# A fused RMSNorm and swish: one small load issued later in ScalarE's queue

## The chip, the cores and the metric

The kernel runs on one core of one Trainium2 chip. The metric is the device time of an execution in microseconds, and a kernel's time is the median of its runs. The profile is of one execution; it has a span (first to last instruction) and an execution time that is a little longer than the span.

## What is computed

The input x has 16 x 1024 rows of 512 numbers in float32, gamma has 512 numbers. Each row is divided by the root of its mean square (plus eps), multiplied by gamma, and passed through swish.

```python
rms = np.sqrt(np.mean(x ** 2, axis=-1, keepdims=True) + eps)
x_norm = x / rms * gamma
return (x_norm * (1.0 / (1.0 + np.exp(-x_norm)))).astype(np.float32)
```

33.6 MB are read and as many written.

## The kernel before

**Tiling.** The 16384 rows are cut into 8 groups of 2048 rows, and each partition (128 of them) has 16 neighbouring rows of a group. A buffer `xb` in on-chip memory holds 6 groups in turn, so groups 6 and 7 take the places of groups 0 and 1. The work on a group goes in chunks of four rows per partition (2048 numbers), 32 chunks in all, counted here from 0. Results are written over the input in `xb` and stored from there.

**Loads.** All but one are issued by SyncE (`load`, line 111), whose DMA queue is called q1 in the profile, in this order: rows 0 to 3 of group 0, rows 4 to 7, rows 8 to 15, then rows 1 to 15 of group 1 (3840 KB), then whole groups (4096 KB) 2 to 6, and group 7 in two halves. The first two are placed ahead of all else in SyncE's program. The load of group 6 waits for the store of group 0, and that of group 7 for the store of group 1. Row 0 of group 1 (one row per partition, 256 KB, 128 pieces of 2 KB) is loaded on its own through ScalarE's DMA queue, q10 (line 185). Its landing is told by the semaphore `s_row`.

**Gamma.** POOL clears `gamma4` (line 131). Then ScalarE issues a DMA (line 187) that brings gamma (8 KB in all) to every 32nd partition, and VectorE spreads it over all partitions with a shuffle (line 228). This shuffle stands behind the first reduce in VectorE's order.

**A chunk k on the engines.** ScalarE waits for the load that holds the chunk, squares one row with an accumulating sum (line 156), and squares the other three rows into one of two PSUM buffers (line 163): this is `square(k)`. Only the first chunk of group 1, which is chunk 4, waits in addition for `s_row`. VectorE sums the three rows (line 204, `sums`). POOL adds eps and raises to the power -1/2 (lines 136 and 143). VectorE multiplies each of four rows by its factor and by gamma (line 215, `norm`). ScalarE applies Silu in place (line 175, `swish`). After the last chunk of a store's piece, ScalarE issues the store through q10 (line 180).

**The order on the engines.** Each engine's order is written out by hand. ScalarE: the row's load, gamma's load, the table load for its functions (line 190), then for each k `square(k)`, the stores that are due, `swish(k - 2)`. A store is due when its last chunk is at most k - 2; so the store of group 6 stands behind `square(30)`, which waits for the last load. VectorE: `sums(0)`, the shuffle of gamma, `sums(1)`, `norm(0)`, and so on: `sums(k)`, `norm(k - 1)`.

Of the kernel before, what the change touches and what calls it, by code (L numbers as in the profile page):

```python
# [9 lines left out]
def kernel(  # L10
# [7 lines left out]
    nc = tc.nc  # L18
# [6 lines left out]
    xf = x.flatten_outer_dims()  # L25
# [50 lines left out]
    s_row = nc.alloc_semaphore("s_row")  # L76
# [12 lines left out]
    def need(ins, sem, value):  # L89
        return ins.wait_op(sem, value, "sem-ge")  # L90

    def dram(ap, piece):
        g, r, n = piece
        rows = ap[g * P * gn : (g + 1) * P * gn]
        return rows.rearrange("(p n) d -> p n d", n=gn)[:, r : r + n, :]

    def buf(piece):
        g, r, n = piece
        at = g % ring * gn + r
        return xb[:, at : at + n, :]  # L100
# [33 lines left out]
    for k in range(K):  # L134
        need(
            nc.gpsimd.tensor_scalar(  # L136
                out=aeps[:, k, :], in0=ms[:, k, :], scalar1=eps_f, scalar2=None,
# [6 lines left out]
                out=rstd[:, k, :], in0=aeps[:, k, :], in1=neg_half, op=ALU.pow  # L144
# [5 lines left out]
    def square(k):  # L150
        at, landing = chunks[k]
        if landing is not None:
            nc.scalar.wait_ge(ld[landing], 16)  # L153
            if loads[landing][1] % cn:
                nc.scalar.wait_ge(s_row, 16)
        acc = nc.scalar.activation(  # L156
            out=junk[k % 2], in_=xb[:, at + n_sq, :], func=AF.Square,
            scale=inv_d**0.5, accum_out=ms[:, k, n_sq : n_sq + 1],
        )
        if k >= 2:  # L160
            need(acc, s_acc, k - 1)
        acc.then_inc(s_acc, 1)
        square = nc.scalar.activation(  # L163
            out=sq[k % 2][:, 0:n_sq, :], in_=xb[:, at : at + n_sq, :],
            func=AF.Square, scale=inv_d**0.5,
        )
        if k >= 2:
            need(square, s_sum, k - 1)
        square.then_inc(s_sq, 1)

    def swish(k):
        at, _ = chunks[k]
        rows = xb[:, at : at + cn, :]
        need(
            nc.scalar.activation(out=rows, in_=rows, func=AF.Silu), s_norm, k + 1  # L175
        ).then_inc(s_swish, 1)

    def store(t):
        need(
            nc.scalar.dma_start(out=dram(of, stores[t]), in_=buf(stores[t])),  # L180
            s_swish, ends[t],
        ).then_inc(st[t], 16)

    first_row = (1, 0, 1)
    nc.scalar.dma_start(out=buf(first_row), in_=dram(xf, first_row)).then_inc(s_row, 16)
    need(
        nc.scalar.dma_start(out=gamma4[0:P:32, :], in_=gamma.partition_broadcast(4)),
        s_zero, 1,
# [3 lines left out]
    for k in range(K + 3):  # L192
        if k < K:
            square(k)
        while stored < len(stores) and ends[stored] <= k - 2:
            store(stored)
            stored += 1
        if 2 <= k < K + 2:
            swish(k - 2)
# [74 lines left out]
```

## Time and profile before

| | us |
|---|---|
| median of 6 runs | 160.17 |
| lowest and highest | 160.13 and 161.01 |
| the profiled execution | 160.95 |
| its span | 159.6 |
| DVE, ACT, POOL busy in it | 138.9, 125.2, 65.5 |
| one reduce (line 204), one normalised row (line 215) | 1.75, 0.74 |
| one block of squares (line 163), one swish (line 175) | 1.43, 1.91 |
| row of group 1, issue to landing | 8.4 |
| share of DMA time taken by q10 and by q1 | 49.3% and 49.2% |

The profile is read like this. Engines are named PE (matrix, unused here), DVE (VectorE), ACT (ScalarE), POOL (GpSimd) and SP (SyncE); ACTq and SPq are their queues, which issue DMAs. L204 is line 204 of the kernel. The page gives each engine's busy time, a row of 40 equal slices of the span with a digit of busy tenths each, and the chain of work that ended last, followed back from the last instruction. Other views are the timeline, the list of DMA issues with the time from issue to landing, the waits, and a table of busy time for any stretch of the span. A DMA share of 1.00 means that all 16 DMA engines were moving packets; it can pass 1 since a packet is counted in the stretch where it starts.

### The profile page before, as it was taken

Reading aid. Unit: us, or ns where it says so; the run is one execution under the profiler, and the core shown is the slowest. Engines: PE = TensorE matmul, PEld = TensorE weight load, DVE = VectorE, ACT = ScalarE, POOL = GpSimd, SP = SyncE. Lnnn points to the kernel's source line nnn. Section 1 sums busy time; section 2 is a strip of 40 time slices with the busy share of each in tenths; the row PEclk is TensorE's granted clock in tenths of the full one; section 3 lists DMA queues with packets and bytes.
Section 4 is the critical chain, followed back from the end, with each engine's and each line's share of the span. In section 5 each row is a group of like instructions: output and inputs, shape, how many; then the busy total and the mean of one; then the engine's idle time right before and its main releaser. Section 6 shows DMA issues by size and latency. Waiting matters only on the chain.

```text
span 159.6 us, 435 instructions
## 1 busy us (share of the span) xinstructions
DVE 138.9 (87%) x162; ACT 125.2 (78%) x129; POOL 65.5 (41%) x70
## 2 busy tenths in 40 slices
DVE  0239999999999999999999999999999999699600
ACT  1835888888888889988888888888899886783810
POOL 1034444444455555544444445555554444255000
DMA  7999899999999999999999999999999898999994
GB/s 267 439 413 493 369 517 394 394 394 394 525 396 394 476 437 402 419 484 402 402 495 411 411 452 443 419 435 460 411 402 472 369 509 374 476 419 394 443 406 209
DMA packets 3035, 67.14 MB, mean 421 GB/s; under 512 B 340, under 2 KB 340, under 8 KB 472
## 3 DMA queue, kind: packets, MB, share of 16 engines
q10 hardware_dynamic: 1448, 33.83, 49.3%
q1 hardware_dynamic: 1584, 33.29, 49.2%
q14 instruction: 3, 0.02, 0.0%
HBM read 33.56 MB, written 33.55 MB: 420 GB/s over the span
## 4 chain that ended last, share of the span: by engine, by line
DVE 82%; DMA 6%; ACT 4%; issue 1%; another core or an unknown queue 1%; POOL 0%; ACTq 0%; POOLq 0%
DVE xb L215 51%; DVE ms L204 30%; DMA gamma<-in_gamma_dram 6%; ACT xb L175 2%; ACT sq L163 1%; DVE gamma_sb L228 0%; ACT junk L156 0%; POOL gamma L131 0%; ACTq L153 0%; POOLq L59 0%
## 5 line engine op out<-in xcount | busy, mean ns | idle before, releaser
L215 DVE SCALAR_TENSOR_TENSOR xb<-xb,rstd,gamma_sb 128x512 f32<-128x512 f32 x128 | 87.1, 740 | 0.0
L175 ACT ACTIVATE xb<-xb 128x2048 f32<-128x2048 f32 x32 | 61.1, 1909 | 17.6 <-DVE xb L215 17.6
L204 DVE TENSOR_REDUCE ms<-sq 128x3 f32<-128x1536 f32 x32 | 55.9, 1746 | 8.4 <-ACT sq L163 8.4
L136 POOL TENSOR_SCALAR aeps<-ms 128x4 f32<-128x4 f32 x32 | 20.7, 647 | 77.1 <-DVE ms L204 77.1
L163 ACT ACTIVATE sq<-xb 128x1536 f32<-128x1536 f32 x32 | 45.9, 1433 | 0.0
L143 POOL TENSOR_TENSOR rstd<-aeps,neg_half 128x4 f32<-128x4 f32 x32 | 44.0, 1376 | 2.7
L156 ACT ACTIVATE junk<-xb 128x512 bf16<-128x512 f32 x32 | 19.7, 615 | 5.7 <-DMA xb<-in_x_dram 5.7
L156 ACT ACTIVATION_READ_ACCUMULATOR junk<-xb 128x1 f32 x32 | 6.0, 187 | 0.0
L190 ACT ACT_TABLE_LOAD x1 | 1.3, 1283 | 3.6 <-issue 3.6
L228 DVE LOAD_MASK_SELECT gamma_sb<-gamma x1 | 0.0, 14 | 2.8 <-DMA gamma<-in_gamma_dram 2.8
L131 POOL MEMSET gamma<- 128x512 f32 x1 | 0.5, 524 | 1.5 <-POOLq L59 1.5
L228 DVE STREAM_SHUFFLE gamma_sb<-gamma 128x512 f32<-128x512 f32 x1 | 0.7, 717 | 0.0
L255 POOL MEMSET const-float32-0.0<- 128x1 f32 x1 | 0.1, 98 | 0.2 <-issue 0.2
L255 POOL MEMSET const-uint8-127<- 128x1 uint8 x1 | 0.1, 102 | 0.0
L255 POOL MEMSET const-bfloat16-1.0<- 128x1 bf16 x1 | 0.1, 101 | 0.0
L132 POOL MEMSET neg_half<- 128x4 f32 x1 | 0.1, 101 | 0.0
L255 POOL MEMSET const-float32-1.0<- 128x1 f32 x1 | 0.1, 98 | 0.0
## 6 DMA issues: line engine op xcount, KB each, us to landing
out_dram<-xb ACTq DMA_DIRECT2D x7, 4096.0 KB, 26.4
xb<-in_x_dram SPq DMA_DIRECT2D x5, 4096.0 KB, 50.8
xb<-in_x_dram SPq DMA_DIRECT2D x3, 2048.0 KB, 46.0
out_dram<-xb ACTq DMA_DIRECT2D x2, 2048.0 KB, 8.6
xb<-in_x_dram SPq DMA_DIRECT2D x1, 3840.0 KB, 19.7
xb<-in_x_dram SPq DMA_DIRECT2D x2, 1024.0 KB, 5.9
xb<-in_x_dram ACTq DMA_DIRECT2D x1, 256.0 KB, 8.4
gamma<-in_gamma_dram ACTq DMA_DIRECT2D x1, 8.0 KB
```

What stands on the lines that cost most here:

```text
L131: nc.gpsimd.memset(gamma4, 0.0).then_inc(s_zero, 1)
L132: nc.gpsimd.memset(neg_half, -0.5).then_inc(s_half, 1)
L136: nc.gpsimd.tensor_scalar(out=aeps[:, k, :], in0=ms[:, k, :], scalar1=eps_f, scalar2=None, op0=ALU.add,),
L143: nc.gpsimd.tensor_tensor(out=rstd[:, k, :], in0=aeps[:, k, :], in1=neg_half, op=ALU.pow),
L156: acc = nc.scalar.activation(out=junk[k % 2], in_=xb[:, at + n_sq, :], func=AF.Square, scale=inv_d**0.5, accum_out=ms[:, k, n_sq : n_sq + 1],)
L163: square = nc.scalar.activation(out=sq[k % 2][:, 0:n_sq, :], in_=xb[:, at : at + n_sq, :], func=AF.Square, scale=inv_d**0.5,)
L175: nc.scalar.activation(out=rows, in_=rows, func=AF.Silu), s_norm, k + 1
L190: nc.scalar.preload_act_table_set("silu_and_others")
L204: nc.vector.tensor_reduce(out=ms[:, k, 0:n_sq], in_=sq[k % 2][:, 0:n_sq, :], op=ALU.add, axis=mybir.AxisListType.X,),
L215: ins = nc.vector.scalar_tensor_tensor(out=row, in0=row, scalar=rstd[:, k, j : j + 1], in1=gamma_sb, op0=ALU.mult, op1=ALU.mult,)
L228: nc.vector.stream_shuffle(gamma_sb, gamma4, [0] * 32), s_gld, 16
L255: nc = _bacc.Bacc("TRN2", target_bir_lowering=False, num_devices=1)
```

## The change

ScalarE no longer issues the row's load first of all. It issues it behind `square(0)`, which waits for the landing of the first load; so the row comes behind gamma in the queue q10 and behind that landing in time. The row's bytes, its place, its semaphore and the chunk that waits for it stay as they were. VectorE, POOL and SyncE keep their orders. Three lines are added ahead of `sums`, so that lines from there on are numbered 3 higher, and gamma's load stands on line 186 instead of 187.

```diff
     first_row = (1, 0, 1)
-    nc.scalar.dma_start(out=buf(first_row), in_=dram(xf, first_row)).then_inc(s_row, 16)
     need(
         nc.scalar.dma_start(out=gamma4[0:P:32, :], in_=gamma.partition_broadcast(4)),
         s_zero, 1,
@@
     for k in range(K + 3):
         if k < K:
             square(k)
+        if k == 0:
+            nc.scalar.dma_start(
+                out=buf(first_row), in_=dram(xf, first_row)
+            ).then_inc(s_row, 16)
         while stored < len(stores) and ends[stored] <= k - 2:
             store(stored)
             stored += 1
```

## The prediction

> **What bounds the kernel.** I read the page first. VectorE looks like the limit, since it is busy 87% of the span and the chain that ended last gives it 82%. But the DMA row of the 40 slices is nearly all nines.
>
> ```profile
> span 159.6 us, 435 instructions
> DVE 138.9 (87%) x162; ACT 125.2 (78%) x129; POOL 65.5 (41%) x70
> DMA  7999899999999999999999999999999898999994
> HBM read 33.56 MB, written 33.55 MB: 420 GB/s over the span
> ```
>
> The table of busy time by stretches settles this (per stretch: its length, then DVE, ACT and POOL busy, clock, DMA share, GB/s):
>
> ```profile
> 1.00:34.00 33.00, 24.27 (x29) 23.14 (x27) 12.06 (x14) 1.00 1.02 429
> 36.00:135.00 99.00, 99.00 (x116) 88.50 (x92) 46.88 (x47) 1.00 1.01 433
> 135.00:152.00 17.00, 13.66 (x18) 11.51 (x10) 5.87 (x6) 1.00 0.98 423
> 152.00:153.00 1.00, 0.00 (x0) 0.06 (x1) 0.00 (x0) 1.00 0.85 360
> ```
>
> The 16 DMA engines are full from 1 us to 152, miss about 0.2 us after that, and work to 158. Those 67.1 MB are moved under either kernel. So the end is set by two things: DMA time, which the change cannot shorten, and holes in DMA work, which it can move. The idle time of VectorE at the start is not by itself on the path to the end.
>
> The chain of waits shows where each head start begins and where it dies (start, length, what):
>
> ```profile
> 2.46 8.99 DMA gamma<-in_gamma_dram
> ...
> 11.49 0.72 DVE gamma_sb L228 x2
> ...
> 133.02 1.91 ACT xb L175
> 134.93 1.64 another core or an unknown queue
> ...
> 136.65 0.42 ACT junk L156
> ```
>
> Gamma, 8 KB, takes 8.99 us, and the first normalisation stands behind it. The piece without a name at 134.93 ends at 136.57. That is the landing of the last load (issued at 75.48, 61.1 us to landing in the list of DMA issues); ScalarE waits 1.7 us for it.
>
> **Step 1: gamma lands earlier.** Its issue stays at 2.46, because it waits for POOL's memset (1.90 + 0.52 = 2.42) and not for the row. What is taken away is the row's 128 packets of 2 KB ahead of it in ScalarE's queue (q10):
>
> ```profile
> DMA packets 257, 1.71 MB, mean 428 GB/s; under 512 B 16, under 2 KB 16, under 8 KB 144
> ...
> q1 hardware_dynamic: 129, 1.45, 86.8%
> q10 hardware_dynamic: 128, 0.26, 17.3%
> ```
>
> This is the stretch 5.5 to 9.5 us: all 128 row packets lie in it, and they cost each engine 17.3% of 4 us, 0.69 us. The row, issued at 1.91, thus began 3.6 us later, ended at about 9.3 and landed 1.0 us after that, at 10.3. Gamma alone in the queue, at the same 3.6 us to its first packet and 1.0 us to landing, lands near 7.1. The bounds are 4.5 (the first load, issued at 0.0, had the engines moving after 1.0 us: 2.46 + 1.0 + 1.0) and 11.45 (no gain). Any landing before 8.72 gives the same, since the shuffle stands behind the first reduce (6.96 + 1.76).
>
> **Step 2: the front of the chain.** Shuffle 8.72 to 9.43. The second square block can start near 7.1 instead of 7.50, for the first two loads no longer share with the row: from 5.5 to 7.0 the row took 27.5% of 1.5 us, 0.4 us. Its result is ready at 9.2, so the second reduce runs from 9.43 to 11.1 and the first normalisation starts near 11.1 instead of 13.76: 2.65 us ahead.
>
> Then the loads catch up. The third load lands at 12.89 now; with the row out of part of its way, 0.3 to 0.45 us sooner. Squares then end at 12.6 + 2.06 = 14.65 and the third reduce starts at 14.7 instead of 16.40: 1.7 us ahead. The fourth load (3840 KB, issued at 2.28, 19.7 us) lands at 22.0 under both kernels, as row, gamma and loads up to it are the same bytes on full engines. Its first squares now start at 22.65; they can start at 22.1 at best. They end 2.04 later at 24.14, and the fifth reduce starts at 24.17 instead of 25.03. So of 2.65 us **0.87 us** are left, and no wait on a load follows until 134. The first store goes out near 30.5 instead of 31.40.
>
> **Step 3: the row itself.** It is issued when the first squares have started, near 4.95, beside squares that run until 6.9; its 0.40 us of issue holds nothing, as the next ScalarE instruction waits for the second load. First packets come 3.6 us later (by the row now) or 4.9 (by the first store: issued at 31.40, no q10 packet before 36): 8.5 to 9.9. Eight packets per engine take turns with packets of 0.61 to 1.14 us, at most 8 x 1.22 = 9.8 us; landing at 20.7 at the latest. It is needed at 22.1. I cost this at nothing; the cover is those 1.4 us or more, and a row later than 22.1 would only eat into the 0.87.
>
> The Trainium skill speaks against this step: "DMA: Bandwidth & Descriptors", section "Rules for kernel authors", would have a DMA issued early and waited for late, and the row is now issued 3 us later. By the rule something should be lost; by the margin above, nothing is. The same page's "Latency and other measured facts" gives about 0.6 us to the first byte on such a queue, where this trace shows 3.6 us behind a busy one; by the page gamma would be there near 4, and the sum would be the same, because of the reduce.
>
> **Step 4: what the 0.87 us does at the other end.** From 36 us both queues have work until the last load is in, and share the engines (36 to 40 us: q10 60.6%, q1 36.0%; 36.2 to 135: 56.3 and 44.4). Before that, loads have the engines to themselves. If stores begin d earlier, loads have moved d less and get about half the rate for the rest, so the last load lands about d *later*: 136.57 becomes 137.4. Packets of 32 KB last 1.21 us and take turns, so the true shift may be 0 or one turn, 1.2. From that landing to the last store is fixed work, 152.09 - 136.57 = 15.5 us; so the last store is issued d later, near 153.0.
>
> **What hides that.** At the very end one engine runs behind the others:
>
> ```profile
> 157.00:157.50 0.50, 0.00 (x0) 0.00 (x0) 0.00 (x0) 1.00 1.23 524
> 157.50:158.00 0.50, 0.00 (x0) 0.00 (x0) 0.00 (x0) 1.00 0.09 33
> 158.00:158.30 0.30, 0.00 (x0) 0.00 (x0) 0.00 (x0) 1.00 0.13 55
> 158.30:158.60 0.30, 0.00 (x0) 0.00 (x0) 0.00 (x0) 1.00 0.00 0
> 158.60:159.60 1.00, 0.00 (x0) 0.00 (x0) 0.00 (x0) 1.00 0.04 16
> ```
>
> From 157.5 only a few packets start, the last one alone after 158.6. In the trace's records of landings, 15 of the last store's 16 parts are in by 158.55 and the last at 159.59. The late engine still has the previous store's packets until about 154, so it does not notice a later issue. The 15 others do: they end at 158.55 + d. Hence the span's end is the larger of 159.59 and 158.55 + d: the cover is 1.04 us. With d = 0.87 nothing changes; with d = 1.2 it is +0.16.
>
> **Sum.** Profiled execution: 160.95, that is its span of 159.6 and 1.35 around it; predicted span 159.6 to 159.8. The median of the runs shown is 160.17, which is 0.78 less; if their late engine lags by less, the last load also lands sooner, and the cover stays. I predict 160.17 + 0.08, the middle of 0 and 0.16: **160.25 us**.
>
> **Rivals.**
> *A (forecast, 0.44).* Head start real, cut to 0.87 us by the fourth load, paid back as a later last load, hidden: 160.17 to 160.33.
> *B (slower, 0.36).* The later last load is not hidden: the last store is issued 0.87 or 1.2 us later and the DMA engines stand idle that long just before it (and also ahead of the group 6 store, which is issued behind the same landing). It decides as soon as the shift exceeds the cover; with no cover it costs all of it: 161.0 to 161.4, I take 161.0. For it: the hole at 152 to 153 (0.85) is there already. Against it: the late engine, if unprofiled runs have it.
> *C (faster, 0.12).* The head start reaches the end: 160.17 - 0.87 = 159.3. For it: VectorE has 82% of the chain and no gap from 36 to 135. Against it: DMA shares of 1.02 and 1.01, and a last load that waits for stores to share with.
> *D (does not do what it says, 0.08).* Gamma is late for another reason than the row, d = 0: 160.17.
>
> **Chances.** 0.3% is 0.48 us, about what a measurement of this kernel can tell from no change. Faster 0.12 (C), same 0.52 (A and D), slower 0.36 (B). The range 159.7 to 161.2 leaves out C and the far part of B, about 0.2; the likeliest case's own range is 160.0 to 160.4.
>
> **What would show it.** Gamma's shuffle right behind the first reduce, near 8.7 (step 1); the third reduce near 14.7 and the fifth near 24.2, behind a wait for the fourth load at 22.0 (step 2); the row landed before that (step 3); first store near 30.5, last load landing at 137 or later, last store near 153 (step 4); DMA share below 0.85 around 152 to 153 if B is right. Wrong I would be if the last load landed earlier than 136.5 with an earlier first store, if the row landed after 22, or if the late engine was gone.

## The result, and the profile after

The changed kernel takes 160.93 us (median of 27 runs, 160.34 to 161.58); the kernel before takes 160.43 in the 55 runs that now stand beside it (160.06 to 161.14). The ratio is 1.0025, with an interval of 1.0017 to 1.0034: 0.25% slower, about 0.4 us (the medians themselves lie 0.5 us apart). That is inside the 0.3% that was set as no change, and the interval reaches just past it. 160.25 was forecast, in a range of 159.7 to 161.2. Beside the experiments below, the kernel before has medians of 160.37 to 160.65, so kernels are compared by their ratios. A ratio leaves out runs over 1.5% above the fastest of their kernel; there are two of these, both of the experiment with no load in the way. Single executions of one kernel spread over some 1 us, so a single profile says little about 0.4 us: the profiled execution took 160.83, less than the 160.95 of the one before.

The page's lines after the change, to be set beside those of before:

```profile
span 159.5 us, 435 instructions
...
DVE 139.2 (87%) x162; ACT 125.3 (79%) x129; POOL 65.5 (41%) x70
...
DMA  7999899999999999999999999999999999999887
...
HBM read 33.56 MB, written 33.55 MB: 421 GB/s over the span
```

Bytes are those of before, and busy times and span differ by 0.3 us or less. What has moved is seen in the timeline (start, length, engine and line, operation, idle time before it):

```profile
4.91 0.36 ACTq L195 DMA_DIRECT2D xb<-in_x_dram  x1
...
8.67 0.72 DVE L231 STREAM_SHUFFLE gamma_sb<-gamma 128x512 f32<-128x512 f32 x1
...
14.93 1.76 DVE L207 TENSOR_REDUCE ms<-sq 128x3 f32<-128x1536 f32 x1 [1.07 <-ACT sq L163]
...
22.10 0.63 ACT L156 ACTIVATE junk<-xb 128x512 bf16<-128x512 f32 x1 [0.82 <-DMA xb<-in_x_dram]
...
24.20 1.76 DVE L207 TENSOR_REDUCE ms<-sq 128x3 f32<-128x1536 f32 x1 [0.55 <-ACT sq L163]
...
30.58 0.35 ACTq L180 DMA_DIRECT2D out_dram<-xb  x1
...
153.18 0.34 ACTq L180 DMA_DIRECT2D out_dram<-xb  x1
```

The third reduce, the fifth, the first store and the last were these in the kernel before:

```profile
16.40 1.75 DVE L204 TENSOR_REDUCE ms<-sq 128x3 f32<-128x1536 f32 x1
...
25.03 1.75 DVE L204 TENSOR_REDUCE ms<-sq 128x3 f32<-128x1536 f32 x1
...
31.40 0.35 ACTq L180 DMA_DIRECT2D out_dram<-xb  x1
...
152.09 0.34 ACTq L180 DMA_DIRECT2D out_dram<-xb  x1
```

The shuffle follows the first reduce at once. The head start is 1.5 us at the third reduce (14.93 against 16.40). The wait for the fourth load, new at 22.10, cuts it to 0.83 us at the fifth reduce and 0.82 at the first store. The chain that ended last shows where this leads:

```profile
2.27 19.76 DMA xb<-in_x_dram
...
22.10 0.72 ACT junk L156 x2
...
132.20 1.91 ACT xb L175
134.11 3.55 another core or an unknown queue
...
137.75 0.42 ACT junk L156
```

The chain now starts at the fourth load and not at gamma. ScalarE is ready 0.8 us sooner for the last load (the swish ahead of it starts at 132.20 instead of 133.02) and gets it 1.09 us later, at 137.66 instead of 136.57; it waits 3.55 us where it waited 1.64. The table by stretches shows the hole that follows (DMA share and GB/s last):

```profile
135.00:152.00 17.00, 12.85 (x17) 10.42 (x10) 5.14 (x5) 1.00 0.96 412
152.00:153.00 1.00, 0.00 (x0) 1.00 (x1) 0.00 (x0) 1.00 1.19 508
153.00:154.00 1.00, 0.00 (x0) 0.15 (x1) 0.00 (x0) 1.00 0.12 49
```

In the kernel before, the last of these three stretches was full:

```profile
153.00:154.00 1.00, 0.00 (x0) 0.00 (x0) 0.00 (x0) 1.00 0.96 410
```

A packet is counted where it starts, so 1.19 and 0.12 are read together: 1.31 of two microseconds. Taken by each packet's own start and end in the trace, 0.5 us of these two stands idle on an average engine, against 0.2 before. The last store is issued at 153.18, 1.09 us later than before. The end has changed its form as well:

```profile
157.00:157.50 0.50, 0.00 (x0) 0.00 (x0) 0.00 (x0) 1.00 1.23 524
157.50:158.00 0.50, 0.00 (x0) 0.00 (x0) 0.00 (x0) 1.00 1.23 524
158.00:158.30 0.30, 0.00 (x0) 0.00 (x0) 0.00 (x0) 1.00 0.00 0
158.30:158.60 0.30, 0.00 (x0) 0.00 (x0) 0.00 (x0) 1.00 2.05 874
158.60:159.60 1.00, 0.00 (x0) 0.00 (x0) 0.00 (x0) 1.00 0.01 0
```

Packets start in step up to 158.6, and then none: all 16 engines now end together, where before one worked alone after 158.6.

### The profile page after: what moved, and what is told of

It reads as the page before. It is cut to its first block, busy times and chain, and to the rows that moved or that the text cites. A ratio compares the mean times of both kernels' runs of the same rounds, so it can differ in the third digit from the quotient of the medians.

```text
span 159.5 us, 435 instructions
## 1 busy us (share of the span) xinstructions
DVE 139.2 (87%) x162; ACT 125.3 (79%) x129; POOL 65.5 (41%) x70
## 4 chain that ended last, share of the span: by engine, by line
DVE 75%; DMA 12%; ACT 5%; another core or an unknown queue 2%; issue 0%; SPq 0%; ACTq 0%
DVE xb L218 46%; DVE ms L207 28%; DMA xb<-in_x_dram 12%; ACT xb L175 2%; ACT sq L163 2%; ACT junk L156 1%; SPq L111 0%; ACTq L155 0%; ACTq L153 0%
## 6 DMA issues: line engine op xcount, KB each, us to landing
xb<-in_x_dram ACTq DMA_DIRECT2D x1, 256.0 KB, 11.2
```

## The experiments

**Gamma ahead of the row, both early** (on the kernel before):

```diff
-    nc.scalar.dma_start(out=buf(first_row), in_=dram(xf, first_row)).then_inc(s_row, 16)
     need(
         nc.scalar.dma_start(out=gamma4[0:P:32, :], in_=gamma.partition_broadcast(4)),
         s_zero, 1,
     ).then_inc(s_gld, 16)
+    nc.scalar.dma_start(out=buf(first_row), in_=dram(xf, first_row)).then_inc(s_row, 16)
```

> The kernel before with gamma's load issued ahead of the row's, both ahead of the first squares: the row goes out near 3.5 us instead of 4.9. Theory: gamma lands near 8 as in the changed kernel, the fourth load at 22.0 again leaves about 0.87 us of head start, first store near 30.5, last load at 137.4 to 137.7, time 160.9 as the changed kernel. Rival (the row's wait for the first landing costs, not gamma's place): 160.4, as before.

Measured: 160.85, ratio 1.0026 (1.0015 to 1.0037), as the changed kernel. First store at 30.40, last load at 137.82, last store at 153.33, span 159.7. So it is the place behind gamma that counts, and not the wait for the first landing.

**One more shuffle ahead of the fourth normalisation** (on the changed kernel):

```diff
+        if k == 4:
+            nc.vector.stream_shuffle(spare, gamma4, [0] * 32)
         if k >= 1:
             norm(k - 1)
```

> The changed kernel with one more shuffle of gamma (0.72 us, into a spare buffer nobody reads) on VectorE between the fifth reduce and the fourth block of normalisations, so that the first store goes out at about 31.3 us as in the kernel before, instead of 30.58. Row and gamma stay as in the changed kernel. Theory (the earlier first store pushes the last load back): last load lands near 136.7 to 137.0 instead of 137.66, last store is issued near 152.3 instead of 153.18, time back to 160.4 to 160.6. Rival (the row in its later place costs DMA time among the larger packets): the time stays at 160.9, with the last load at 137.6.

Measured: 160.49, ratio 1.0012 (1.0000 to 1.0024). First store at 31.21, last load at 136.96, last store at 152.48. Row and gamma are as in the changed kernel, and VectorE has 0.7 us *more* to do; the last load comes back by 0.7 us and about half of the 0.25% with it. The intervals overlap, and the second profile of the changed kernel (below) has its last load at 137.11 without any hold, so two single profiles show little here. The counts of executions say more: 4 of 12 take 160.7 us or more, against 8 of 12 for gamma ahead of the row and 22 of 27 for the changed kernel (13 of 55 for the kernel before).

**More head start: group 1 in two halves through SyncE, no row of its own** (on the kernel before; the row's DMA, its semaphore and its wait are taken out):

```diff
-    loads += [(1, 1, gn - 1)] + [(g, 0, gn) for g in range(2, G - 1)]
+    loads += [(1, 0, 8), (1, 8, 8)] + [(g, 0, gn) for g in range(2, G - 1)]
```

> The kernel before without the row's load of its own: group 1 comes whole through SyncE's queue, in two halves of 2048 KB, so that nothing stands ahead of gamma and the fifth chunk needs only the first half (landing near 17.5 us instead of 22.0). The head start is then cut by the third load alone, to about 1.7 us. Theory (an earlier first store pushes the last load back, uncovered from about 0.6 us on): first store near 29.7, last load near 138.4, last store issued near 153.9, time 161.5 to 161.9. Rival (the cost saturates, as the DMA engines are full anyway): 160.4 to 160.9, not above the changed kernel.

Measured: 164.02, ratio 1.0207 (1.0175 to 1.0239). First store at 29.30, last load at 141.05, last store at 156.56, span 162.9. The sign and the place are as the theory has them, and the size is above it. Its stretches:

```profile
139.00:140.00 1.00, 0.33 (x1) 0.00 (x0) 0.00 (x0) 1.00 0.23 98
140.00:141.00 1.00, 0.00 (x0) 0.00 (x0) 0.00 (x0) 1.00 0.08 33
141.00:142.00 1.00, 0.00 (x0) 0.87 (x3) 0.00 (x0) 1.00 0.00 0
142.00:156.00 14.00, 11.37 (x14) 10.17 (x8) 4.09 (x4) 1.00 1.01 431
156.00:157.00 1.00, 0.00 (x0) 0.53 (x1) 0.00 (x0) 1.00 0.62 262
```

For most of three microseconds the DMA engines have nothing to do: 15 of the 16 parts of the last load are in by 138.96 and the last one only at 141.05, the stores issued so far are done or nearly so, and the store of group 6 stands on ScalarE behind the wait for the last load (it is issued at 141.21). The last load came 4.5 us later for a first store 2.1 us earlier. One us of this is the one late part: it is 2.09 us behind the other 15, where it was 1.05 behind in the kernel before. The other 3.4 us are common to all parts. The 32 KB load packets were also slower: above their usual 1.21 us they took 1.9 us per engine in all, against 0.7 before. Why, and what makes up what still remains, is open.

**No load in the way at all** (as the last one, and):

```diff
-    loads = [(0, 0, 4), (0, 4, 4), (0, 8, 8)]
+    loads = [(0, 0, 4), (0, 4, 4), (0, 8, 4), (0, 12, 4)]
```

> As the run with group 1 in halves, and the third load (rows 8 to 15 of group 0) is cut in two as well, so that no load cuts the head start: about 2.65 us. Theory: first store near 28.8, last load near 139.3, last store issued near 154.8, time 162.3 to 162.8. Rival (saturation): 160.4 to 160.9. Rival (a VectorE that is ahead shortens the time): 159 or less.

Measured: ratio 1.0225 (1.0172 to 1.0278), profiled execution 163.75; the six runs lie between 163.26 and 169.38, wider apart than those of any other kernel here. First store at 28.77, last load at 140.54, last store at 156.06, span 162.4; DMA share from 139 to 142 is 0.41. The price is not seen to grow further with the head start (the intervals of the two overlap), but it is far above that of the changed kernel.

**The same, held back** (as the last one, and four more shuffles at the place of the first hold):

> As the run with no load in the way, with four more shuffles of gamma (0.72 us each, into spare buffers nobody reads) on VectorE ahead of the fourth block of normalisations, so that the first store goes out near 31.5 as in the kernel before. Theory: last load near 136.6, time 160.3 to 160.6, in spite of the cut loads. Rival (the cut loads themselves cost): as the run without the hold.

Measured: 160.72, ratio 1.0010 (0.9988 to 1.0033). First store at 31.43, last load at 136.95, last store at 152.46. With the same cut loads, 2% come back when VectorE is made to do four shuffles more, which take 2.5 us from 24.23 to 26.73. This is the strongest single finding: a large head start of VectorE costs time here. The hold moves all later work with the first store; the next experiment moves the first store alone.

**The first store one chunk later** (on the changed kernel):

```diff
-        while stored < len(stores) and ends[stored] <= k - 2:
+        while stored < len(stores) and ends[stored] <= k - (3 if stored == 0 else 2):
```

> The changed kernel with the first store alone issued one chunk later, near 34.9 us instead of 30.58. Theory: the last load lands about 4 us earlier, near 133.5, ScalarE no longer waits for it, VectorE works without a gap from 24 us, the last store is issued near 149.8, the hole in DMA work at 153 goes, and the DMA engines alone set the end: 159.9 to 160.2. Rival (a store that goes out later is paid at the end): 161 or more. Rival (the time follows VectorE): 157.5.

Measured: 160.69, ratio 1.0006 (0.9994 to 1.0019). The store went out at 32.81 and not 34.9: the squares that stand ahead of it in ScalarE's order start only at 34.62, so the issue did not wait for them. The last load landed at 134.67, 3.0 us earlier than in the changed kernel for a first store 2.2 us later, and ScalarE waited 0.8 us for it; the last store was issued at 150.19, the DMA share from 153 to 154 is 1.00. The profiled execution took 160.23, with a span of 158.9, but the ratio is that of before and the median is not the 159.9 to 160.2 expected: without a late last load, DMA work alone gives no better time than the kernel before has.

**The first store in two pieces, the first earlier** (on the kernel before):

```diff
-    stores = [(g, 0, gn) for g in range(G - 1)]
+    stores = [(0, 0, 12), (0, 12, 4)] + [(g, 0, gn) for g in range(1, G - 1)]
```

> The kernel before with the store of group 0 cut in two, 12 rows per partition issued near 27.1 us and 4 rows at 31.4, so that stores begin 4.3 us earlier. Theory: the last load lands 3 to 4.3 us later, near 140, the last store is issued as much later, and of that only what the late engine covers is hidden: 163 to 164.7. Rival (the DMA engines are full anyway, so the order of loads and stores does not matter): 160.4.

Measured: 160.60, ratio 1.0014 (1.0003 to 1.0026): a miss. Stores began at 27.11, yet the last load landed *earlier*, at 131.35. The DMA queues between 50.2 and 62 us show a likely reason (packets, MB, share of time):

```profile
q1 hardware_dynamic: 121, 3.83, 75.3%
q10 hardware_dynamic: 131, 1.24, 24.6%
```

The queues take turns by packet, about one for one. The piece of 4 rows has packets of 8 KB, which give its queue a quarter of the time, where whole stores got 56% between 36.2 and 135 us in the kernel before. The Trainium skill says this of turns ("DMA: Bandwidth & Descriptors", section "Queues, rings and completion order": each engine goes round its queues packet by packet), and the counts of this trace fit, 131 packets to 121. The edit changed two things at once and does not test what it was made for.

**The last store in two pieces** (on the changed kernel):

```diff
-    stores += [(G - 1, 0, 8), (G - 1, 8, 8)]
+    stores += [(G - 1, 0, 8), (G - 1, 8, 4), (G - 1, 12, 4)]
```

> The changed kernel with its last store (8 rows per partition) cut in two stores of 4 rows, the first issued one chunk earlier, near 150.5, the second near 153.2 as now. Row, gamma, first store and last load stay as in the changed kernel (last load near 137.7). Theory (the end is the later of two things: DMA work, and the last store's issue plus the 6.3 us that it takes): the hole in DMA work at 153 to 154 closes, the last store now takes some 4 us, DMA work alone sets the end, span 158.9 to 159.5 and time 160.3 to 160.6. Rival (the cost of the change lies in the DMA work of the start or the middle): the time stays at 160.9.

Measured: 160.81, ratio 1.0015 (1.0003 to 1.0026). The hole at 153 is nearly gone (0.85), the last load is at 137.57; the span is 159.5. Less came back than expected.

**The cut last store with the late first store:**

> As the run with the cut last store, with the first store issued one chunk later as well, so that the last load lands near 134.7 and nothing waits for it. Theory: DMA work alone sets the end, as in the run with the late first store: 160.2 to 160.7, no gain over the kernel before. Rival (the lateness of the last store still counts something): below 160.2.

Measured: 160.62, ratio 1.0001 (0.9987 to 1.0015), span 159.3. No gain over the kernel before, as expected; so cutting the last store costs nothing by itself.

**The cut last store, and the store of group 6 ahead of the last wait** (on the changed kernel with the cut last store):

```diff
+        if k == K - 2:
+            store(stored)
+            stored += 1
         if k < K:
             square(k)
```

> As the run with the cut last store, and the store of group 6 is issued ahead of the squares that wait for the last load, near 134 us instead of 137.7, so that the stores do not run dry at 138 either. First store and row as in the changed kernel. Theory (the cost of the change is only the holes in DMA work behind the last load): no second of DMA work below full from 2 us to 157, ratio to the kernel before 1.000 to 1.001, time 160.4 to 160.7, though the last load may land later still, near 138. Rival (the cost lies elsewhere, as the cut last store alone gave back only part): ratio 1.0015 to 1.0025 again.

Measured: 160.96, ratio 1.0021 (1.0006 to 1.0035): a miss, and an important one. Its profile has no hole left to speak of behind the last load, its lowest share from 137 to 154 being 0.93:

```profile
2.00:137.00 135.00, 127.80 (x148) 113.60 (x119) 61.12 (x62) 1.00 1.01 430
137.00:138.00 1.00, 0.00 (x0) 0.76 (x3) 0.00 (x0) 1.00 0.99 426
138.00:139.00 1.00, 0.00 (x0) 1.00 (x1) 0.00 (x0) 1.00 1.22 524
139.00:152.00 13.00, 11.37 (x14) 9.17 (x8) 4.09 (x4) 1.00 0.97 418
152.00:153.00 1.00, 0.00 (x0) 0.64 (x1) 0.00 (x0) 1.00 0.98 418
153.00:154.00 1.00, 0.00 (x0) 0.00 (x0) 0.00 (x0) 1.00 0.93 393
```

That execution has a span of 159.0 and took 160.35, the shortest of 12, and the median is 160.96. So with the first store at 30.63, an edit that closes the holes in the execution that was profiled did not bring the median back. Whether they were closed in the longer executions too, no profile shows.

**Both kernels profiled again.** Before:

> The kernel before once more, for another profile of it. Theory: the late DMA engine of the first profile (one of 16 landings 1.04 us behind the rest, span 159.6) is not the same in every execution; a span nearer 159.1 goes with a lag below 0.8 us, and the last load then lands at 136.3 or sooner. Rival: the lag is fixed at 1.04.

Span 159.6, time 160.92; one engine is again alone at the end, 1.08 us behind, last load at 136.56. The rival was right as far as two profiles go, but both are of long executions, and the theory is about shorter ones. The profiles of the other kernels bear it out. Where DMA work sets the end, the last part of the last store is 0.04 to 0.30 us behind the other 15 in the four profiles with spans of 158.9 to 159.3 (first store later, in two pieces, and the two with a cut last store beside a later first store or an earlier store of group 6). It is 0.62 to 1.08 behind in the five with spans of 159.5 to 159.8. After:

> The changed kernel once more, for another profile of it. Theory: last load near 137.7, last store issued near 153.2, span 6.3 us after that, near 159.5, with the DMA share between 153 and 154 far below 1. Rival: the hole is an accident of the first profile.

Span 158.9, time 160.25, last load at 137.11, last store at 152.62, 6.3 us ahead of the end; the DMA share from 153 to 154 is 0.66. The relation held, and the level was 0.6 us lower than in the first profile. Here too one late engine makes most of the difference: the first 15 parts of the last load are in at 136.89 and 136.92, the last one 0.22 us later in this profile and 0.74 in the first.

| kernel | first store | last load landed | last store | span | ratio to before |
|---|---|---|---|---|---|
| first store later | 32.81 | 134.67 | 150.19 | 158.9 | 1.0006 |
| before | 31.40 | 136.57 | 152.09 | 159.6 | 1 |
| before, second profile | 31.57 | 136.56 | 152.08 | 159.6 | - |
| all early, held | 31.43 | 136.95 | 152.46 | 159.8 | 1.0010 |
| after, held | 31.21 | 136.96 | 152.48 | 159.6 | 1.0012 |
| after, second profile | 30.52 | 137.11 | 152.62 | 158.9 | - |
| after | 30.58 | 137.66 | 153.18 | 159.5 | 1.0025 |
| gamma, then row | 30.40 | 137.82 | 153.33 | 159.7 | 1.0026 |
| group 1 in halves | 29.30 | 141.05 | 156.56 | 162.9 | 1.0207 |
| all early | 28.77 | 140.54 | 156.06 | 162.4 | 1.0225 |

In every row the last store follows the last load by 15.5 us. In the last five rows the end follows the last store by 6.3 us; in the first five it comes 7.1 to 8.7 us after it, and DMA work sets it. The times are of one profile each, and two profiles of one kernel lie up to 0.55 us apart, so only the differences of several microseconds stand by themselves.

## Why the prediction was right, and where it was not

**Steps 1 and 2 held.** Gamma was issued at 2.45 and its shuffle ran at 8.67; the first normalisation started at 11.13 (11.1 forecast), the third reduce at 14.93 (14.7: the third load landed some 0.2 us later than I took it), the fourth load at 22.0, the fifth reduce at 24.20 (24.17), the first store at 30.58 (30.5). The head start of 2.6 us shrank to 0.83. Within these steps three terms were off, and other waits hid them. Three of gamma's four parts landed by 7.22 (7.1 forecast), but the fourth at 8.31, 0.4 us before the shuffle. The second and the third load came 0.13 and 0.14 us sooner, where 0.4 and 0.3 to 0.45 were taken. The first reduce and the shuffle covered the first two, and the fourth load took away what the third would have given. That part is luck.

**Step 3 held.** The row was issued at 4.91 and landed 11.2 us later, at 16.1, six microseconds ahead of its need. So breaking the rule of the Trainium skill that was weighed there ("DMA: Bandwidth & Descriptors", section "Rules for kernel authors") has no price here: with gamma ahead of a row issued at 3.59, the ratio is the same (1.0026 against 1.0025).

**Step 4 held in direction and roughly in size** for this change: in the first profiles the last load is 1.09 us later, in the second 0.55 (0.87 or one turn of 1.2 were given), and the last store was issued at 153.18 and 152.62 (153.0). For a bigger head start the size was far too small: 4.5 us came of 2.1.

**The term that was mis-sized is the cover.** In the profile the span is as forecast: a cover of 1.04 us against a shift of 1.09 gives 159.64, and 159.5 was measured. The end has another form than was thought, though: the late engine, whose absence I had named as a sign of being wrong, is gone there (0.02 us behind in both profiles). And I carried the cover over to the median with the sentence that a smaller lag would leave it as it is, and there 0.4 us came through where 0 to 0.16 was given. The two profiles of before, 160.95 and 160.92, lie 0.5 us above the median of its runs, while the profiles of after lie 0.1 and 0.7 below its own: the cover was measured on executions that are late by more than is usual.

Of the 0.68 us between 160.25 and 160.93, 0.26 is the level: six runs gave 160.17 for the kernel before, 55 give 160.43. The rest is the change, 0.4 to 0.5 us where 0.08 was added, and that is a third to a half of what rival B gives with no cover. That it still counts as no change owes something to where the limit of 0.3% was set.

**What stays open** is what carries the 0.25% in the usual execution. Both profiles of the changed kernel show rival B's mechanism, a later last load and a hole behind it. The held kernels and the later first store show that the time of the first store sets the landing of the last load, and for the large head starts the time of the kernel. But the edit that closes the holes did not bring the median back, so for this small change the holes are not shown to be the whole of it. Nor do the profiles show a cost: their spans are 158.9 and 159.5, against 159.6 twice before. What differs is how many executions are long: 13 of 55 before the change and 22 of 27 after it take 160.7 us or more. Leaving out the kernels with the large head starts, each profiled execution of 160.7 us or more has one engine that lags by 0.6 us or more, and the shorter ones 0.3 us or less (at the last load where the end follows the last store by 6.3 us, at the last store elsewhere). Whether the change makes that happen more often, nothing here shows. For the large head starts, with about two empty microseconds between 139 and 142 and spans of 162.4 and 162.9, the holes make up most of it.

Rival C is out: in no run did a head start of VectorE end in a shorter time. Rival D is out: gamma did come sooner, by 2.8 us at the shuffle.

No version beat the kernel before: the best, with a late first store and a cut last one, is at 1.0001.

## What to carry to other kernels

In this kernel the DMA engines are full nearly from end to end, and there a compute engine's head start was worth nothing and could cost: it starts the stores earlier, these share the engines with loads that are still queued, and the last load, which the tail hangs on, lands later. So look at what an edit does to the first store and the last load before counting the stall that it removes. And when the effect is as small as this one, 0.25% where single executions spread over 0.7%, a cover read from one profile is a term with a spread of its own; set the profiled time beside the median before using it.

## What the hardware did that was not expected

A queue whose store has packets of 8 KB got a quarter of the DMA time beside loads with packets of 32 KB (24.6% against 75.3%), and with the store of group 0 cut into a large and a small piece the last load landed 5 us earlier (131.35 against 136.57), with the time 0.14% longer. The DMA issue of a store went out before instructions that stand ahead of it in ScalarE's order had begun: moved back by one chunk of 4.3 us, the first store was issued only 2.2 us later (32.81 against 30.58), ahead of squares that start at 34.62. And one of the 16 parts of a load or store can trail the other 15 by up to 2.09 us, differently from one execution to the next of the same program (0.74 and 0.22 us at the last load of the changed kernel).
